# A decoder step on one core: where VectorE's low parts stand beside side work, and when TensorE's side steps are issued

## The chip, the core and the metric

The kernel runs on one core of one Trainium2 chip. The metric is the device time of one execution in microseconds (us), the median of several runs. The core's engines run side by side, each through its own queue in order: TensorE (PE in the profile; PEld is its weight load), VectorE (DVE), ScalarE (ACT), GpSimd (POOL) and SyncE (SP), which here only starts transfers. An instruction that waits holds up whatever stands behind it in the same queue.

## The reference, cut to what matters

One layer of a hybrid decoder for 256 prompt tokens and 8 x 4 sample tokens (288 in all), width 2048, in fp32:

```python
mkv = rms_norm(mem_prompt, mem_norm_g) @ w_mem_kv            # keys and values of 256 memory tokens
h = rms_norm(x, norm_g)
c_h, c_b, c_c, c_g, q, n_g, b_g, kv6, m_q, m_g = split_cols(h @ w_in)
y_a = silu(c_g) * short_conv_mixer(c_h, c_b, c_c, conv_prev, w_conv)
# 8 query heads, 2 key groups: compressed, selected and sliding-window attention
o_cmp, o_sel = nsa_cmp_sel(q, q_rot, pos, k_cmp, v_cmp, k_sel, v_sel)   # sample: over 2048 cached rows
y_b = silu(n_g) * (g0 * o_cmp + g1 * o_sel + g2 * o_win)
y_m = silu(m_g) * gqa_attend(m_q, mem_k, mem_v)              # 4 heads over the memory
x = x + concatenate([y_a, y_b, y_m]) @ w_out
y = rms_norm(x, final_g)
```

The new key and value rows, the convolution state and the updated windows are outputs too.

## The kernel before, in words

**The weight products.** Columns of a weight matrix are taken 128 at a time; each such tile has 16 blocks of 128 rows and is cut into two *halves* of 8 blocks (128 x 1024 numbers, 512 KB). There are 152 halves (`NH`): 16 of `w_mem` (the first four multiply raw fp32, the `zf` products, `DIRECT = 4`), 104 of `w_in`, and 32 of `w_out` in two passes of 16. The *first output pass* (halves 120 to 135) takes the rows that belong to convolution and memory attention (`y1a`, `y1b`); the *last pass* (halves 136 to 151) takes those of the sparse attention (`y`), and there each half is a whole product.

To keep fp32 precision a half `s` is split: ScalarE copies it to a *high part* `wh` (`w_hi`), VectorE subtracts that from the raw half and writes the *low part* `wl` (`w_lo`). A half then takes 24 matmuls into a PSUM tile `z` (two buffers): 8 with `wh` times the high part of the tokens, 8 with `wh` times their low part, 8 with `wl`; they are sorted so that `wl` is wanted from the 17th on (in halves 4 and 5 earlier). Raw halves have 5 buffers (`WR`), high parts 3, low parts 2. A raw buffer is free once its low part is written, and then GpSimd's queue starts the load of a later half (`w_load`, `LOAD_AT`). So `wl` of half s+2 can be written only when the matmuls of half s are over.

**Side work.** Everything else (norms, rotary embedding, convolution, gates, all attention, pooling of the cached rows, outputs) is written as Python generators. `chunk()` runs after every 12 matmuls of a half and once after each product; it advances each generator in the list `live` to its next `yield`. `yield 1` means the next chunk, `yield 2` the one after. All engines' queues are thereby written out in one order by hand, ahead of time.

**The planner.** While the program is written, `at[0]` adds up estimates for TensorE, `at[VEC]` and `at[ACT]` for the other engines' work, `at[1]` for transfers. `until(i)` lets a generator go on only when `at[0]` has passed the end of engine `i`'s work so far by `WAIT`. `behind(i, j)` puts one engine's clock behind another's and issues nothing. These estimates steer the order alone; what runs is governed by semaphores.

**The stream of cached rows.** `stage_stream` takes the stages in a fixed order as their tiles arrive: `cmp_use` (pooling one tile: a multiplication shared by VectorE and GpSimd, then a sum `pooled` on VectorE; 64 of them), `selk_use` and `wink_use` (scores `sk`), `memk_use` (scores `smd`), `memv_use` (`omd`), `winv_use` and `selv_use` (outputs `od`). `cmp_use` is held back while VectorE's clock is more than `BACKLOG` ahead of TensorE's. `selk_use` waits for the flag `q`, `memk_use` for `mq`. Six buffers `st` (and later one more, `qk`) hold the tiles.

**Steps that the change and the prediction name.** `first_tiles` runs the first four halves and splits the memory tokens (`m`); `mem_tile` scales `z` into `mvt`; `prep_x` normalises and splits the tokens. `dec_cmp` makes compressed scores (`sc`) and, from `S`, the block importances (`imp`); `dec_softmax` builds `odr` from `S` and transposes it (`pe`); `dec_out` and `mem_out` transpose the collected outputs (`ot`, `otm`). `prompt_cmp` makes the prompt's compressed scores (`kcps`, `scp`, `scpt`) and weights `pc`, which `prompt_nsa` transposes (`pct`) before its own softmax `P` and its transposition `pt`. `split_y1` makes the inputs of the first output pass once `prompt_done` and `mem_decoded` are set, `split_y2` and `split_decode` those of the last; if they are not there, the program idles.

In the last pass `second_pass` adds `z` to `ysum` on VectorE, squares it on ScalarE (`ysq`), adds the square to `yacc` on VectorE and scales `ysum` on ScalarE; `residual` adds the input `xr` meanwhile. For half s the queues hold, in this order, ScalarE: `wh` of s+2, then square and scale of s; VectorE: `wl` of s+2, then the sum and the accumulation of s.

Of the kernel before, what the change touches and what calls it, by code (L numbers as in the profile page):

```python
# [47 lines left out]
C_SEL = C_NS + 32  # L48
CS = C_SEL + 2048
CMP_LAG = 2  # L50
WAIT = 0.2
BACKLOG = 2.5
NST = 6

T_C0, T_C1, T_K0, T_V0 = (24, 94), (94, 185), (67, 113), (128, 162)
# [12 lines left out]
LOAD_AT = 21  # L68
DIRECT = 4
WARM = 5  # L70
TAIL_BUSY = (5, 7)
OUT_PIECES = (1, 2, 2, 3, 3, 3, 2)

# [2 lines left out]
def decode_step(ctx, tc, xT, xN, memT, cst, w_in, w_mem, w_out, w_bg, pt, ptv, ckc, ckk, ckv, wk, wv, mk, mv,  # L76
# [22 lines left out]
    VEC, ACT, SYNC = 2, 3, 4  # L99
# [38 lines left out]
    def behind(i, j):  # L138

        at[i] = max(at[i], at[j])  # L140
# [79 lines left out]
    def w_hi(s):  # L220
        if DIRECT <= s < NH and s not in his:
            his[s] = pw.tile([128, 1024], F32R, name=f"wh{s}", tag="wh", bufs=WH)
            act.activation(his[s], raws[s], AF.Copy)
# [18 lines left out]
    def product_half(out, hi, lo, first, last):  # L242
        s = nhalf[0]
        nhalf[0] += 1
        w_hi(s + 2)
        wh, wl = his.pop(s), los.pop(s)
        mm = []
        for j in range(8):
            a = wh[:, j * 128:(j + 1) * 128]
            mm += [(j, a, hi(j)), (j + (0 if s > DIRECT + 1 else 4), a, lo(j)), (j + 8, wl[:, j * 128:(j + 1) * 128], hi(j))]  # L250
        mm.sort(key=lambda x: x[0])
        for n, (_, a, b) in enumerate(mm):
            if s == DIRECT and n == 0:
                w_load(s + WR)
            if n == LOAD_AT:
                w_load(s + WR + 1)
            matmul(out, a, b, start=(first and n == 0), stop=(last and n == 23))
            if n == 23:
                w_lo(s + 2)
            if n % 12 == 11 and not (last and n == 23):  # L260
                chunk()
# [3 lines left out]
    def first_tiles():  # L265


        z = [pz.tile([128, 512], F32, name=f"zf{i}", tag="z")[:, :256] for i in range(2)]
        for k0 in (0, 8):
            for i in range(2):  # L270
                s = nhalf[0]
                nhalf[0] += 1
                w_hi(s + 2)
                w_lo(s + 1)
                w = raws[s]
                for j in range(8):
                    matmul(z[i], w[:, j * 128:(j + 1) * 128], m_g(k0 + j, 1)[:, 0], start=(k0 + j == 0), stop=(k0 + j == 15))
                    if j == 7:
                        w_load(s + WR)
                        first_loads(s)  # L280
                        if s == DIRECT - 1:
                            w_lo(s + 2)
                    if j == 3 or j == 7 and k0 == 0:
                        chunk()
                if i == 1:
                    for k in (k0, k0 + 4):
                        vec.tensor_tensor(m_hl[1][:, k:k + 4, :], m_g(k, 4), m_hl[0][:, k:k + 4, :].bitcast(F32),
                                                op=ALU.subtract)
                if k0 == 8:
                    yield z[i]  # L290
# [78 lines left out]
    def dec_cmp(hf):  # L369

        yield from until(VEC)
        while ("S", hf) not in env or hf and "first" not in env:
            yield 1
        t = ptr.tile([128, 512], F32, name=f"kcT{hf}", tag="t")
        matmul(t[:, :256], wcmp[:, 0], pooled[hf][:, 0].rearrange("p g q b n -> p (g q b n)"), start=True, stop=True)
        kcT = zt("A", "kcT")[:, :256].rearrange("p (g n) -> p g n", g=2)
        vec.tensor_copy(kcT.rearrange("p g n -> p (g n)"), t[:, :256])
        yield 1
        t = ptr.tile([128, 512], F32, name=f"vc{hf}", tag="t")
        for g in range(2):  # L380
            matmul(t[:, g * 128:(g + 1) * 128], pooled[hf][:, 1, g].rearrange("p q b n -> p (q b n)"), wcmp[:, 1], start=True, stop=True)
        act.activation(Vc, t[:, :256], AF.Copy)
        yield 1
        S = env["S", hf]
        s = pss.tile([128, 512], F32, name=f"sc{hf}", tag="s")
        for g in range(2):
            for b in range(4):
                matmul(s[32 * b:32 * b + 32, 0:32], qcols(1, 4 * hf + b, g), kcT[:, g].rearrange("p (q b n) -> p q b n", q=8, b=4)[:, :, b, :],
                                 start=(g == 0), stop=(g == 1), skip_group_check=True)
        mx, nm, sm = small(1, "mx1"), small(1, "nm1"), small(1, "sm1")  # L390
        vec.tensor_reduce(mx, s[:, 0:32], axis=AX.X, op=ALU.max)
        vec.tensor_scalar(nm, mx, -SCALE, None, op0=ALU.mult)
        yield 1
        act.activation(S[:, 0:32], s[:, 0:32], AF.Exp, scale=SCALE, bias=nm, accum_out=sm)
        yield 1
        vec.reciprocal(sm, sm)
        vec.tensor_scalar(S[:, 0:32], S[:, 0:32], sm, None, op0=ALU.mult)
        yield 1
        t = ptr.tile([128, 512], F32, name=f"imp{hf}", tag="t")
        matmul(t[:, 0:32], C("rep"), S[:, 0:32], start=True, stop=True)  # L400
        imp = small(32, "imp", 1)
        vec.tensor_copy(imp, t[:, 0:32])
        yield 1
        v8, v16 = small(8, "v8"), small(8, "v16")
        iv = imp[:, 1:31]
        vec.max(v8, iv)
        vec.match_replace(iv, v8, iv, -2.0)
        vec.max(v16, iv)
        vec.memset(v16[:, 5:8], -3.0)
        vec.match_replace(iv, v16, iv, -2.0)  # L410
        madd = small(32, "madd", 1)
        vec.tensor_scalar(madd, imp, -1.0, NEG, op0=ALU.is_ge, op1=ALU.mult)
        vec.memset(madd[:, 0:1], 0.0)
        vec.memset(madd[:, 31:32], 0.0)
        env["madd", hf] = madd
        spawn(dec_softmax(hf), 1)
# [48 lines left out]
    def dec_softmax(hf):  # L465
# [32 lines left out]
        for a, b, m in ((C_NS, h, 1), (h, CS, 1), (C_WIN, C_NS, 2)):  # L498
            vec.tensor_scalar(S[:, a:b], S[:, a:b], sm[:, m:m + 1], None, op0=ALU.mult)
            if m == 1:  # L500
# [5 lines left out]
        vec.tensor_tensor(X.rearrange("p (q b n) -> p q b n", q=8, b=4),  # L506
                                S[:, 0:32].rearrange("p (q n) -> p q n", q=8).unsqueeze(2).to_broadcast([128, 8, 4, 4]),
                                C("bsel").unsqueeze(1).unsqueeze(3).to_broadcast([128, 8, 4, 4]), op=ALU.mult)
        yield 1
        t = ptr.tile([128, 512], F32, name=f"pe{hf}", tag="t")  # L510
        transpose(t[:, 0:128], X, ident)
        env.pop("odr")
# [64 lines left out]
    def dec_out(hf):  # L577
        yield from take("odr")
        o = env.pop("o")
        mg = C("mg")  # L580
        r = small(128, "odr", 1)
        vec.tensor_scalar(r, o[:, 0:128], mg[:, 0:1], None, op0=ALU.mult)
        vec.scalar_tensor_tensor(r, o[:, 128:256], mg[:, 1:2], r, op0=ALU.mult, op1=ALU.add)
        yield 2
        t = ptr.tile([128, 512], F32, name=f"ot{hf}", tag="t")
        transpose(t[:, 0:128], r, ident)
        env.pop("odr")
        a, b = 256 + 16 * hf, 272 + 16 * hf
        act.activation(mixed[:, 8:16, a:b].rearrange("p h (b t) -> p h b t", t=4),
                             t[:, 0:128].rearrange("p (b h t) -> p h b t", b=4, t=4), AF.Copy)  # L590
        env["decoded", hf] = True
# [65 lines left out]
    def mem_out():  # L657
        yield from take("odr")
        o, mh = env["mo"], C("mh")
        env.pop("o")  # L660
        r = small(128, "odr", 1)
        vec.tensor_scalar(r, o[:, 0:128], mh[:, 0:1], None, op0=ALU.mult)
        for h in range(1, 4):
            vec.scalar_tensor_tensor(r, o[:, h * 128:(h + 1) * 128], mh[:, h:h + 1], r, op0=ALU.mult, op1=ALU.add)
        yield 2
        t = ptr.tile([128, 512], F32, name="otm", tag="t")
        transpose(t[:, 0:128], r, ident)
        env.pop("odr")
        act.activation(mixed[:, 4:8, 256:NT].rearrange("p h (b t) -> p h b t", t=4),
                             t[:, 0:128].rearrange("p (b h t) -> p h b t", b=8, t=4), AF.Copy)  # L670
        env["mem_decoded"] = True
# [313 lines left out]
    def q_tile(h, z):  # L985
# [12 lines left out]
        if hh == 3:  # L998
            yield 1
            yield from rope_out(put)  # L1000
        if h == 7:
            env["q"] = True

    pool_p = one.tile([128, 2, 2, 4], F32, name="pool_p")
# [36 lines left out]
    def mq_tile(h, z):  # L1041
        act.activation(mq[:, h, :], z[:, :256], AF.Copy)
        sv = z[:, 256:NT].rearrange("p (c b t) -> p c b t", b=2, t=4)
        for b2 in range(2):
            o = b2 * 16 + h * 4
            vec.tensor_copy(qmz[:, :, b2, h, o:o + 4], sv[:, :, b2, :])
        if h == 3:
            env["mq"] = True
        return
        yield  # L1050
# [104 lines left out]
    def prompt_cmp():  # L1155
# [12 lines left out]
        v = vcp.rearrange("p g d -> p (g d)")  # L1168
        act.activation(v, t[0:96, 128:384], AF.Copy)
        vec.tensor_tensor(v[32:64], t[32:64, 128:384], v[32:64].bitcast(F32), op=ALU.subtract)  # L1170
        yield 2

        s = pss.tile([128, 512], F32, name="scp", tag="s")
        for i in range(4):
# [1 line left out]
                   stop=True, skip_group_check=True)  # L1176
        sT = pbig.tile([128, 1024], F32, name="scpT", tag="big")
        act.activation(sT[:, :512], s, AF.Copy)
        yield 1
        t = ptr.tile([128, 512], F32, name="scpt", tag="t")  # L1180
        for i in range(4):
            transpose(t[:, i * 128:(i + 1) * 128], sT[:, i * 128:(i + 1) * 128], ident)
# [19 lines left out]
        for a in range(2):  # L1202
            vec.tensor_tensor(pc3[:, a], pc[:, a].unsqueeze(1).to_broadcast([128, 3, 8, 4]),
                                    smv[:, a].unsqueeze(1).unsqueeze(3).to_broadcast([128, 3, 8, 4]), op=ALU.mult)
        yield 1

    def prompt_nsa(g, tt):
        L = 128 * (tt + 1)
# [351 lines left out]
```

## Time and profile before

| | before |
|---|---|
| runs, us | 641.89, 642.78, 643.66 (median 642.78) |
| profiled execution, us | 642.73, of which the span of instructions is 641.0 |
| granted TensorE clock | 0.99 |
| TensorE busy | 609.3 us, 95% of the span |
| VectorE busy | 457.5 us, 71% |
| ScalarE busy | 287.9 us, 45% |
| GpSimd busy | 206.8 us, 32% |
| moved by DMA | 188.40 MB, mean 294 GB/s |

How to read the lines that follow: a line of the order of time gives start and length in us, engine, line of the kernel, operation, tiles (written `<-` read), shape and count, and in brackets how long the engine had been idle before it and what ended that. Matmuls are pipelined, so a line of 16 of them overlaps the next. A line of waits gives the total in us, how many, and the longest. A line of stretches gives for each engine the busy time and the number of instructions, then the granted clock of TensorE, the share of the DMA engines in use and GB/s.

The stages by time: memory projection to 67 us (with the tokens' preparation in 40 to 64), queries, keys and values, convolution and gates with all attention beside them to 508 us, first output pass to 569 us, last pass to 628 us, final norm and output to the end.

### The profile page before, as it was taken

To read this page: it belongs to the slowest core of one execution; us is meant where nothing else is said; L and a number is where in the kernel's file an instruction comes from. 1 tells how busy PE (TensorE), PEld (TensorE's weight loads), DVE (VectorE), ACT (ScalarE), POOL (GpSimd) and SP (SyncE) were. 2 spreads that over 40 slices of the span, in tenths; PEclk is the share of its full clock that TensorE was granted. 3 is DMA by queue.
4 is the path that set the end of the run, shared out by engine and by line. 5 is a ranking of instruction groups with operands and counts; after the bars stand their busy time and mean duration, and the time that the engine had idled before them with its cause. 6 is when DMAs were issued, how large, how long until landed. Compare 5 with 4: busy or idle time off the path is not lost. (4 is left out here: it accounts for less than half of the span.)

```text
span 641.0 us, 13356 instructions
## 1 busy us (share of the span) xinstructions
PE 609.3 (95%) x4895; PEld 561.3 (88%) x4895; DVE 457.5 (71%) x735; ACT 287.9 (45%) x500; POOL 206.8 (32%) x288
## 2 busy tenths in 40 slices
PE   7899999999999999889999899999999999999983
PEld 5799999989999899878898789988889889999973
DVE  3769799979587679677786978977586443447554
ACT  4656444454454434233334443445434343435550
POOL 1122554534236433232364452322103343122100
PEclk9999999999999999889999999999999999999998
DMA  8999698999999997877778899898979997488703
GB/s 260 360 404 399 211 359 303 337 328 327 314 286 357 383 379 264 327 249 259 266 281 269 292 342 296 295 321 293 372 265 341 336 300 291 152 299 261 230 4 147
DMA packets 74627, 188.40 MB, mean 294 GB/s; under 512 B 8945, under 2 KB 25842, under 8 KB 74178
## 3 DMA queue, kind: packets, MB, share of 16 engines
q0 software_dynamic: 27232, 105.10, 46.7%
q1 hardware_dynamic: 46320, 81.17, 36.4%
q10 hardware_dynamic: 1010, 1.28, 0.5%
q8 instruction: 38, 0.62, 0.4%
q14 instruction: 27, 0.22, 0.1%
HBM read 182.31 MB, written 13.60 MB: 306 GB/s over the span
## 5 line engine op out<-in xcount | busy, mean ns | idle before, releaser
L133 DVE TENSOR_TENSOR wl<-w,wh 128x1024 fp32r<-128x1024 f32 x148 | 184.4, 1247 | 110.9 <-PE z L116 50.9
L116 PE MATMUL z<-x,wh 128*128 128x288 f32 x1664 | 258.4, 304 | 0.4 <-ACT wh L133 0.4
L116 PEld LDWEIGHTS z<-x,wh 128*128 128x128 f32 x1664 | 232.5, 190 | 9.2 <-issue 6.9
L133 ACT ACTIVATE wh<-w 128x1024 fp32r<-128x1024 f32 x148 | 154.6, 1051 | 24.0 <-PE z L116 17.6
L116 PE MATMUL z<-x,wl 128*128 128x288 f32 x832 | 127.0, 295 | 0.2 <-DVE wl L133 0.2
L116 PEld LDWEIGHTS z<-x,wl 128*128 128x128 f32 x832 | 115.7, 188 | 0.4 <-DVE wl L133 0.4
L341 POOL TENSOR_TENSOR st<-st,cst 128x512 f32<-128x512 f32 x56 | 63.0, 1126 | 129.2 <-issue 55.3
L217 POOL DMA_DIRECT2D w<-w_in x104 | 58.3, 560 | 93.6 <-DVE wl L133 73.3
L133 DVE TENSOR_REDUCE pooled<-st 128x16 f32<-128x1024 f32 x56 | 67.8, 1211 | 8.6 <-POOL st L341 8.6
L116 PE MATMUL z<-y,wh 128*128 128x288 f32 x256 | 37.8, 299 | 3.5 <-DVE ysum L133 3.5
L133 DVE TENSOR_TENSOR st<-st,cst 128x512 f32<-128x512 f32 x56 | 39.0, 699 | 2.7 <-DMA st<-ckc 2.7
L561 POOL DMA_INDIRECT st<-ckv,rows_v x29 | 30.6, 1055 | 31.4 <-PE od L116 14.9
L116 PEld LDWEIGHTS z<-y,wh 128*128 128x128 f32 x256 | 34.8, 188 | 5.7 <-issue 5.6
L217 POOL DMA_DIRECT2D w<-w_out x32 | 17.6, 553 | 61.2 <-DVE wl L133 57.7
L116 PE MATMUL z<-y1a,wh 128*128 128x288 f32 x224 | 35.4, 298 | 0.0
L116 PEld LDWEIGHTS z<-y1a,wh 128*128 128x128 f32 x224 | 31.8, 188 | 1.6 <-issue 1.2
L116 PE MATMUL z<-m,wh 128*128 128x256 f32 x192 | 27.4, 287 | 3.3 <-DVE m L133 1.6
L133 ACT ACTIVATE P<-P,nm 128x128 f32<-128x128 f32 (+1 forms) x32 | 14.2, 444 | 32.2 <-DVE nm L133 32.2
L116 PEld LDWEIGHTS z<-m,wh 128*128 128x128 f32 x192 | 24.5, 191 | 4.5 <-issue 1.9
L133 ACT ACTIVATE ysum<-z 128x288 f32<-128x288 f32 x16 | 6.6, 412 | 32.1 <-PE z L116 32.1
L133 ACT ACTIVATE se<-z 128x288 f32<-128x288 f32 x16 | 6.6, 412 | 31.2 <-PE z L116 31.2
L116 PE MATMUL sk<-st,qz 128*32 128x256 f32 x288 | 19.8, 382 | 0.0
(274 smaller groups left out, 715.0 us busy)
## 6 DMA issues: line engine op xcount, KB each, us to landing
w<-w_in POOLq DMA_DIRECT2D x104, 512.0 KB, 6.2
st<-ckc SPq DMA_DIRECT2D x112, 256.0 KB, 6.0
w<-w_out POOLq DMA_DIRECT2D x32, 512.0 KB, 5.1
st<-ckk SPq DMA_DIRECT2D x112, 128.0 KB, 5.2
w<-w_mem POOLq DMA_DIRECT2D x11, 512.0 KB, 9.1
o_wk<-wk POOLq DMA_DIRECT2D x8, 512.0 KB, 6.3
o_wv<-wv POOLq DMA_DIRECT2D x8, 512.0 KB, 6.6
qk<-ckc SPq DMA_DIRECT2D x16, 256.0 KB, 6.4
```

What stands on the lines that cost most here:

```text
L116: nc.tensor.matmul(out, a, b, **kw)
L133: return getattr(self.engine, name)(*args, **kw)
L217: (nc.gpsimd if s >= WR else nc.sync).dma_start(raws[s], wsrc[s])
L341: done.append(eng.tensor_tensor(tm[:, :, kv], tm[:, :, kv], acmp[:, kv].unsqueeze(1).unsqueeze(1).to_broadcast([128, 2, 4, 64]), op=ALU.mu ...
L561: nc.gpsimd.indirect_dma_start(t, None, ckv, bass.IndirectOffsetOnAxis(ap=rows_v[:, j * 4 + b:j * 4 + b + 1], axis=0))
```

## The change: what it does

1. *Low parts.* Before, `wl` of half s+2 is issued right after the last matmul of half s, ahead of the side work of that chunk. Now this holds only for s from 22 (`LOW_FIRST`) to 133 (`NH - 18`, not included). Every half begins with `w_lo(s + 1)`, which does nothing if that part is there; so in halves before 22 and from 134 on, the low part is issued one product or chunk later, behind the side work. The extra call at the end of the four direct halves is gone.
2. *Waits for estimates.* Ten places where a generator went on after one or two chunks now use `until`: in `dec_cmp` before `sc` and before `imp`, in `dec_softmax` before `pe`, in `dec_out` and `mem_out` before the transposition, in `prompt_cmp` before `scp`, before `scpt` and at its end (before `pct`), and before the flags `q` and `mq` are set. Two `behind` lines chain the clocks around an exponential.
3. *Constants.* `WAIT` goes from 0.2 to 0.8, `BACKLOG` from 2.5 to 1.6.

```diff
-WAIT = 0.2
-BACKLOG = 2.5
+WAIT = 0.8
+BACKLOG = 1.6
...
+LOW_FIRST = 22
...
 def product_half(out, hi, lo, first, last):
         w_hi(s + 2)
+        w_lo(s + 1)
         wh, wl = his.pop(s), los.pop(s)
...
-            if n == 23:
+            if n == 23 and LOW_FIRST <= s < NH - 18:
                 w_lo(s + 2)
             if n % 12 == 11 and not (last and n == 23):
                 chunk()
...
 def first_tiles():
                         first_loads(s)
-                        if s == DIRECT - 1:
-                            w_lo(s + 2)
...
 def dec_cmp(hf):
         act.activation(Vc, t[:, :256], AF.Copy)
-        yield 1
+        yield from until(VEC)
...
         yield 1
+        behind(ACT, VEC)
         act.activation(S[:, 0:32], s[:, 0:32], AF.Exp, scale=SCALE, bias=nm, accum_out=sm)
         yield 1
+        behind(VEC, ACT)
         vec.reciprocal(sm, sm)
         vec.tensor_scalar(S[:, 0:32], S[:, 0:32], sm, None, op0=ALU.mult)
-        yield 1
+        yield from until(VEC)
         t = ptr.tile([128, 512], F32, name=f"imp{hf}", tag="t")
...
 def dec_softmax(hf):                       # after odr, before pe
-        yield 1
+        yield from until(VEC)
...
 def dec_out(hf) and mem_out():             # after odr, before ot and otm
-        yield 2
+        yield from until(VEC)
...
 def q_tile(h, z):
         if h == 7:
+            yield from until(VEC)
             env["q"] = True
...
 def mq_tile(h, z):
         if h == 3:
+            yield from until(VEC)
             env["mq"] = True
...
 def prompt_cmp():
         vec.tensor_tensor(v[32:64], t[32:64, 128:384], v[32:64].bitcast(F32), op=ALU.subtract)
-        yield 2
+        yield from until(VEC)
...
         act.activation(sT[:, :512], s, AF.Copy)
-        yield 1
+        yield from until(ACT)
...
                                     smv[:, a].unsqueeze(1).unsqueeze(3).to_broadcast([128, 3, 8, 4]), op=ALU.mult)
-        yield 1
+        yield from until(VEC)
```

More of the change, by code (lines that the diff above doesn't have):

```diff
@@ L1170, in prompt_cmp @@
         vec.tensor_tensor(v[32:64], t[32:64, 128:384], v[32:64].bitcast(F32), op=ALU.subtract)
-        yield 2
+        yield from until(VEC)
         s = pss.tile([128, 512], F32, name="scp", tag="s")
@@ L1204, in prompt_cmp @@
                                     smv[:, a].unsqueeze(1).unsqueeze(3).to_broadcast([128, 3, 8, 4]), op=ALU.mult)
-        yield 1
+        yield from until(VEC)
     def prompt_nsa(g, tt):
```

## The prediction

> **What bounds the kernel now.** I read the busy shares and the clock row of the page first, then who TensorE waited for, then stretches cut at the stages, and last the order of time around each wait.
>
> ```profile
> span 641.0 us, 13356 instructions
> PE 609.3 (95%) x4895; PEld 561.3 (88%) x4895; DVE 457.5 (71%) x735; ACT 287.9 (45%) x500; POOL 206.8 (32%) x288
> PEclk9999999999999999889999999999999999999998
> ```
>
> TensorE carries the span, so only what stops or slows it counts; VectorE has room on the whole. The clock digits fall to 8 in two slices of the middle, which is taken up below. Who TensorE waited for (total us, times, longest):
>
> ```profile
> PE z L116 <- DVE ysum L133: 3.5, 10, 1.7
> PE pe L121 <- DVE odr L133: 3.1, 1, 3.1
> PE pt L121 <- DVE P L133: 2.6, 2, 2.0
> PE pct L121 <- DVE pc L133: 2.0, 1, 2.0
> PE imp L116 <- DVE S L133: 1.7, 2, 1.2
> PE z L116 <- DVE m L133: 1.6, 1, 1.6
> PE z L116 <- DVE mvt L133: 0.9, 1, 0.9
> ```
>
> Each of these waits is for VectorE, although VectorE is not full: work that TensorE needs stands behind other work in its queue. By stage (stretch, length, then PE busy and instructions; the last three figures are clock, DMA share, GB/s):
>
> ```profile
> 24.20:67.20 43.00, 40.08 (x334) 37.62 (x335) 33.98 (x56) 27.27 (x42) 10.69 (x20) 1.00 1.00 373
> 150.00:508.30 358.30, 348.83 (x2918) 316.49 (x2917) 270.07 (x453) 152.72 (x289) 125.50 (x166) 0.99 0.88 308
> 508.30:569.20 60.90, 60.90 (x527) 56.67 (x527) 25.51 (x28) 26.39 (x41) 19.73 (x28) 1.00 0.75 254
> 585.30:627.60 42.30, 38.44 (x271) 36.13 (x271) 23.80 (x36) 22.66 (x36) 5.02 (x10) 1.00 0.40 130
> ```
>
> The idle time of TensorE lies in three places: 2.9 us in the tokens' preparation, 9.5 us in the long middle, 3.9 us in the last pass. The first output pass (508 to 569) has none.
>
> **The change, term 1: the last pass.** Its order of time:
>
> ```profile
> 572.46 2.33 PE L116 MATMUL z<-y,wh 128*128 128x288 f32 x16
> 575.66 2.29 PE L116 MATMUL z<-y,wh 128*128 128x288 f32 x16
> ...
> 585.21 0.44 ACT L133 ACTIVATE ysq<-ysum 128x288 f32<-128x288 f32 x1 [1.66 <-DVE ysum L133]
> 585.32 2.36 PE L116 MATMUL z<-y,wh 128*128 128x288 f32 x16
> 585.68 0.54 ACT L133 ACTIVATE ysum<-ysum,cst 128x288 f32<-128x288 f32 x1
> 586.13 1.04 ACT L133 ACTIVATE wh<-w 128x1024 fp32r<-128x1024 f32 x1
> 587.20 1.23 DVE L133 TENSOR_TENSOR wl<-w,wh 128x1024 fp32r<-128x1024 f32 x1 [0.69 <-ACT wh L133]
> 588.35 0.45 DVE L133 TENSOR_TENSOR ysum<-z,ysum 128x288 f32<-128x288 f32 x1
> 588.94 2.34 PE L116 MATMUL z<-y,wh 128*128 128x288 f32 x16 [0.21 <-DVE ysum L133]
> 623.04 1.83 PE L116 MATMUL z<-y,wh 128*128 128x288 f32 x12 [1.69 <-DVE ysum L133]
> 625.26 0.83 PE L116 MATMUL ssqy<-cst,yacc 128*128 128x1 f32 x6 [0.39 <-DVE yacc L133]
> ```
>
> Undisturbed, a half tile takes 575.66 - 572.46 = 3.20 us. From 585.32 it takes 588.94 - 585.32 = 3.62 us, and that is a ring over two engines: square (ysq), scale, high part (wh) on ScalarE, then low part (wl), sum (ysum) on VectorE, then the next square. It closes because the low part of two halves ahead is issued before the sum of this half, and the sum frees the z buffer that TensorE wants. From 585.32 to 623.04 there are ten halves in 37.72 us; ten at 3.20 are 32.0, so the ring costs 5.7 us. (1.69 us of it is one wait, where ScalarE loads a table.)
>
> From half 134 on the change issues the low part at the start of the next half, behind sum, square and accumulation. The ring is then cut: the sum waits for TensorE alone. What VectorE does for one half, after the product's end:
>
> ```profile
> L133 DVE TENSOR_TENSOR yacc<-yacc,ysq 128x288 f32<-128x288 f32 x14 | 6.4, 457 | 5.2 <-ACT ysq L133 5.1
> L133 DVE TENSOR_TENSOR ysum<-ysum,xr 128x864 f32<-128x864 f32 x4 | 4.2, 1048 | 0.0
> ```
>
> Sum 0.45, then accumulation 0.46 behind the square of 0.44, then the low part 1.23: about 2.7 us with hand-overs, and some 3.1 us in the four halves with a residual addition of 1.05, part of which runs beside the square. Both are under 3.20, and the low part is needed only after 16 matmuls (2.1 us) of the half after the next. ScalarE has 0.44 + 0.54 + 1.04 = 2.0 us a half, and once the table load (the wait of 1.69 us is its mark), which a whole half of lead covers. Behind the later low part stands the weight load in GpSimd's queue, for that raw buffer; it is wanted four halves (12.8 us) on and takes 5.1 us:
>
> ```profile
> w<-w_out POOLq DMA_DIRECT2D x32, 512.0 KB, 5.1
> ```
>
> Without that lead it would cost up to 3 us a half. The extra piece in the last half (ssqy, 0.39 us of waiting) stays, and may grow by 0.2, since the last accumulation then ends about 1.6 us after the product before, when TensorE arrives there. Term 1: -5.7 + 0.2 = **-5.5 us**.
>
> **Term 2: steps that wait for estimates, and WAIT and BACKLOG.** No instruction is added; ten steps that came one or two chunks after their VectorE or ScalarE work (a chunk is 12 matmuls, 1.6 us) now also wait until the planner's clock of that engine is passed by 0.8 us, and the steps that had this already wait 0.8 instead of 0.2. The largest case:
>
> ```profile
> 257.71 1.21 DVE L133 TENSOR_REDUCE pooled<-st 128x16 f32<-128x1024 f32 x1
> 258.84 0.33 DVE L133 TENSOR_TENSOR odr<-S,cst 128x128 f32<-128x128 f32 x1
> 259.22 0.33 PE L121 MATMUL pe<-cst,odr 128*128 128x128 f32 x1 [3.11 <-DVE odr L133]
> ```
>
> The transposition pe was issued one chunk after odr, which stood behind pooling work. Two chunks later it finds odr ready, and the 3.11 us are filled with projection matmuls. The same holds for pct (2.0) behind a chain of small operations that the planner does count. The granted clock tells what else these two waits cost:
>
> ```profile
> 260.00:265.00 5.00, 5.00 (x29) 5.00 (x28) 1.49 (x3) 2.73 (x4) 0.53 (x1) 0.66 1.04 404
> 280.00:285.00 5.00, 2.96 (x20) 2.75 (x19) 4.90 (x13) 2.19 (x5) 1.61 (x2) 0.89 0.68 243
> 285.00:290.00 5.00, 5.00 (x32) 4.98 (x31) 3.40 (x5) 2.09 (x4) 2.12 (x3) 0.77 0.72 235
> 620.00:624.00 4.00, 2.31 (x18) 2.10 (x17) 2.18 (x4) 2.24 (x5) 0.00 (x0) 1.00 0.00 0
> ```
>
> Behind the wait of 3.1 us the clock is 0.66 over 5 us: 1.7 us lost. Behind the wait of 2.0 us it is 0.89 and 0.77: 0.55 + 1.15 = 1.7 us lost. The wait of 1.69 us in the last pass (620 to 624) lowers nothing. So both go with their waits: 3.4 us. The Trainium skill, "TensorE: Matmul & The Clock Gate", Part 1 (What's actually happening), puts the fall to half rate behind at least one whole idle window of about 3.4 us; by that neither wait would be long enough, the 3.4 us would not come back with them, and the sum would be 629.9 instead of 626.5. The trace disagrees for the wait of 2.0 us, so the rows decide.
>
> At most this term holds 3.1 + 2.0 + 1.7 + 2.6 + 3.4 = 12.8 us. I take pe, pct and their clock whole (8.5), 1.2 of imp (one of its two waits follows a VectorE stall that no estimate of VectorE knows), and half of pt (1.3), which was guarded at 0.2 already and waited all the same: 11.0 us. Against it, all side work behind moves to other places and meets other queues. That is not in the trace; between nothing and the whole 12.8 us again, I take 1.5 us, nearest to pt, where guarded steps still waited 2.6 us in all. Term 2: **-9.5 us**.
>
> The lateness itself (a step one or two chunks later, pooling held back by BACKLOG, the flags q and mq set later) I cost at nothing: TensorE always has projection matmuls to put in its place. The cover ends where the first output pass needs its split inputs:
>
> ```profile
> 502.78 0.21 DVE L133 TENSOR_TENSOR y1b<-mixed,y1a 128x64 fp32r<-128x64 f32 x1
> L116 PE MATMUL z<-y1a,wh x224: 288/295/402, 508.4 to 567.9; 128*128 128x288 f32 x112
> ```
>
> The last split ends 503.0, the pass starts 508.4: 5.4 us, three chunks of lateness; each chunk beyond costs 1.6 us.
>
> **Term 3: the tokens' preparation (halves before 24).** Here too the low part goes behind side work.
>
> ```profile
> 27.42 1.22 DVE L133 TENSOR_TENSOR wl<-w,wh 128x1024 fp32r<-128x1024 f32 x1 [1.45 <-ACT wh L133]
> 28.56 2.35 DVE L133 TENSOR_TENSOR m<-mixed,m 128x1024 fp32r<-128x1024 f32 x2
> 29.83 1.22 PE L116 MATMUL z<-m,wh 128*128 128x256 f32 x8 [1.64 <-DVE m L133]
> ```
>
> The low part of half 5 waited 1.45 us for its high part and held up m. Behind m, it lets m start at 27.42 - 1.45 = 25.97, and the wait of 1.64 goes; the low part then ends at 25.97 + 2.35 + 1.22 = 29.5, while TensorE wants it at about 29.2, so 0.4 us come back: -1.2. The wait for mvt (0.9) may shrink too, but DMA is full here (share 1.00 above) and earlier TensorE asks for weights earlier. Bounds -2.5 (both gone) and +1 (low parts late for GpSimd's weight loads, the size of mvt). I take **-1.2 us**.
>
> **Sum.** The profiled execution took 642.73 us (span 641.0), the median of the runs 642.78, so one base serves. 642.7 - 5.5 - 9.5 - 1.2 = **626.5 us**.
>
> **Rivals.**
> - *All waits go*: 642.7 - 5.7 - 12.8 - 2.5 = 621.7. For it: every wait has a guard now. Against: imp and pt.
> - *The middle's waits come back elsewhere*: term 2 is nothing, 642.7 - 5.5 - 1.2 = 636.0. For it: the same VectorE work must be done, and pt was guarded and waited.
> - *Too few z buffers, not the order*: the last pass keeps its 3.62 us, 626.5 + 5.5 = 632.0. For it: TensorE's wait there is for a buffer that ysum frees. Against: the first output pass uses the same two buffers at 3.2 us a half with no idle time. The Trainium skill, "Perfetto Trace Analysis", Identifying Performance Opportunities, reads a gap that repeats on the busy engine as a sign of too few buffers; the trace speaks for the order.
> - *The low clock has another cause*: 626.5 + 3.4 = 629.9.
> - *Slower*: the guarded chain to the memory outputs comes so late that the first output pass waits for its inputs. Slower than 644.7 it becomes once the 16.2 us are used up and 2 more: 18.2 / 1.6 = 11 chunks beyond the three that are free. Two or three late steps stand in that chain, so it would take pooling held back for some 20 us.
> - *The guards do nothing* (estimates already past) and the ring re-forms at 3.6 us: within 0.3% of 642.8.
>
> **Chances.** Forecast 0.60, all gone 0.10, middle back 0.14, buffers 0.05, clock 0.03, no change 0.03, slower 0.05. Faster by over 0.3% (about 2 us, what this kernel's measurement can tell) sums to 0.92, within it 0.03, slower 0.05. The range for 8 in 10 reaches from 621.0 (all gone, a little over) to 636.5 (middle back).
>
> **What would show it.** Last pass: halves at 3.20 us to the end, no TensorE wait for ysum, wl behind yacc on VectorE. Middle: no waits of pe and pct and no half-rate clock before the end. Early: no wait for m. Wrong it would be if TensorE idles between the gates and the first output pass, if waits for P or sk grow, or if the last pass stays above 3.4 us a half.

## The result, and the profile after

The changed kernel takes 626.16 us (median of 4 runs, 624.2 to 627.6) against 643.22 us before (4 runs): a ratio of 0.9735, 95% interval 0.9701 to 0.977. Run again later, beside other runs of the kernel before (641.96 us), it took 623.90 us, ratio 0.9735 (0.9699 to 0.977). The forecast was 626.5.

The page of the profiled execution (625.25 us in all):

```profile
span 622.8 us, 13340 instructions
PE 604.3 (97%) x4895; PEld 558.4 (90%) x4895; DVE 458.2 (74%) x735; ACT 287.2 (46%) x500; POOL 209.4 (34%) x288
PEclk9999999999999999999999999999999999999997
```

VectorE does the same 735 instructions in the same time; TensorE is idle less, and the clock digits have no 8 in the middle any more. Who TensorE waited for (total us, times, longest):

```profile
PE z L117 <- ACT wh L134: 2.2, 3, 1.2
PE sk L117 <- DMA st<-ckk: 2.2, 3, 1.2
PE zeros L117 <- POOL zeros L783: 1.1, 1, 1.1
PE zf L117 <- DVE mixed L134: 1.0, 2, 0.8
PE zf L117 <- DMA w<-w_mem: 1.0, 1, 1.0
PE acc L117 <- ACT cu L134: 0.5, 1, 0.5
PE z L117 <- DVE wl L134: 0.5, 2, 0.3
```

All seven waits that the prediction listed are gone (ysum, odr, P, pc, S, m, mvt). The waits for zeros, mixed and w_mem stand at the very start and were there before (1.1, 1.7 and 1.6 us). What came in is smaller: 1.9 of the 2.2 us for wh (0.4 was there before), 2.2 for the transfer of sk's rows, 0.5 for acc and 0.3 for wl. Where the time went, by the stages' own marks: four stretches from the first split product to the first token product, to the first output pass, to the last pass, to its last `wl` matmuls; first before, then after (stretch, length, then the engines' busy times in the order PE, PEld, DVE, ACT, POOL, then clock, DMA share, GB/s).

```profile
24.25:67.24 42.99, 40.11 (x334) 37.66 (x335) 33.93 (x56) 27.26 (x42) 10.68 (x19) 1.00 1.00 373
67.24:508.40 441.16, 431.07 (x3547) 396.85 (x3546) 345.51 (x566) 192.20 (x356) 164.16 (x214) 0.99 0.89 309
508.40:569.25 60.85, 60.85 (x527) 56.62 (x526) 25.51 (x28) 26.39 (x41) 19.62 (x28) 1.00 0.75 254
569.25:627.50 58.25, 54.38 (x392) 51.97 (x391) 34.27 (x49) 29.91 (x47) 8.38 (x16) 1.00 0.55 182
```

```profile
22.27:64.10 41.83, 39.69 (x337) 37.49 (x337) 34.72 (x59) 27.34 (x42) 11.18 (x20) 1.00 1.03 392
64.10:496.67 432.57, 429.14 (x3546) 394.20 (x3545) 345.45 (x564) 191.72 (x356) 166.40 (x213) 1.00 0.90 316
496.67:557.42 60.75, 60.75 (x527) 56.52 (x526) 26.40 (x29) 26.22 (x41) 20.04 (x29) 1.00 0.76 252
557.42:609.30 51.88, 51.88 (x391) 51.72 (x390) 33.39 (x48) 29.88 (x47) 8.35 (x16) 1.00 0.63 207
```

The preparation is 1.2 us shorter, the middle 8.6, the first output pass 0.1, the last pass 6.4. Another 2.0 us stand ahead of the first mark (24.25 to 22.27), where both kernels wait, among other things, for their first transfers; in the eleven other profiles that mark lies between 22.9 and 25.2, with the early part of the change and without it, so these 2 us belong to the execution and not to the change. Together 18.2 us between these two profiled spans, 17.1 between the medians.

The last pass in order of time, one half:

```profile
567.04 2.29 PE L117 MATMUL z<-y,wh 128*128 128x288 f32 x16
567.24 0.46 DVE L134 TENSOR_TENSOR ysum<-z,ysum 128x288 f32<-128x288 f32 x1 [0.27 <-PE z L117]
567.73 0.45 ACT L134 ACTIVATE ysq<-ysum 128x288 f32<-128x288 f32 x1 [1.23 <-DVE ysum L134]
568.21 0.46 DVE L134 TENSOR_TENSOR yacc<-yacc,ysq 128x288 f32<-128x288 f32 x1 [0.51 <-ACT ysq L134]
568.59 1.22 DVE L134 TENSOR_TENSOR wl<-w,wh 128x1024 fp32r<-128x1024 f32 x1
570.24 2.29 PE L117 MATMUL z<-y,wh 128*128 128x288 f32 x16
605.44 1.76 PE L117 MATMUL z<-y,wh 128*128 128x288 f32 x12
607.12 0.83 PE L117 MATMUL ssqy<-cst,yacc 128*128 128x1 f32 x6
```

The sum now waits for TensorE, not the reverse. From 567.04 to 605.44 there are twelve halves in 38.40 us, 3.20 each, to the end, and the extra piece ssqy is reached without a wait for yacc.

### The profile page after: what moved, and what is told of

It reads as the page before. It is cut to its first block, busy times and chain, and to the rows that moved or that the text cites. A ratio compares the mean times of both kernels' runs of the same rounds, so it can differ in the third digit from the quotient of the medians.

```text
span 622.8 us, 13340 instructions
## 1 busy us (share of the span) xinstructions
PE 604.3 (97%) x4895; PEld 558.4 (90%) x4895; DVE 458.2 (74%) x735; ACT 287.2 (46%) x500; POOL 209.4 (34%) x288
## 4 chain that ended last, share of the span: by engine, by line
PE 83%; DMA 10%; DVE 3%; ACT 1%; issue 1%; SPq 1%; ACTq 0%; DVEq 0%
PE z L117 67%; DMA st<-ckk 4%; PE od L117 3%; DMA st<-xN 2%; PE sk L117 2%; PE acc L117 2%; PE s L117 1%; DMA mraw<-memT 1%; DMA st<-ckc 1%; DMA qk<-ckk 1%; PE pv L122 1%; DVE ysum L134 1%; DMA rows_v<-ptv 1%; PE pt L122 1%; PE omd L117 1%
## 5 line engine op out<-in xcount | busy, mean ns | idle before, releaser
L117 PE MATMUL z<-x,wh 128*128 128x288 f32 x1664 | 255.1, 302 | 0.4 <-ACT wh L134 0.4
L117 PEld LDWEIGHTS z<-x,wh 128*128 128x128 f32 x1664 | 229.9, 188 | 9.5 <-issue 7.3
L341 POOL TENSOR_TENSOR st<-st,cst 128x512 f32<-128x512 f32 x56 | 64.8, 1160 | 117.5 <-issue 55.4
L218 POOL DMA_DIRECT2D w<-w_out x32 | 17.5, 551 | 58.6 <-DVE wl L134 44.8
L117 PE MATMUL sk<-st,qz 128*32 128x256 f32 x288 | 21.6, 382 | 2.2 <-DMA st<-ckk 2.2
L117 PE MATMUL z<-y,wl 128*128 128x288 f32 x128 | 19.6, 295 | 0.0
```

Of the source, the lines that this page charges most:

```text
L117: nc.tensor.matmul(out, a, b, **kw)
L218: (nc.gpsimd if s >= WR else nc.sync).dma_start(raws[s], wsrc[s])
L341: done.append(eng.tensor_tensor(tm[:, :, kv], tm[:, :, kv], acmp[:, kv].unsqueeze(1).unsqueeze(1).to_broadcast([128, 2, 4, 64]), op=ALU.mu ...
```

## The experiments

All are compared with runs of the kernel before on the same chip, taken together with them. Single executions of one kernel lie up to 5 us from their median here, so differences under 2 us are read from the traces, each of which shows one execution.

**The parts alone.** First the last pass only:

```diff
         w_hi(s + 2)
+        w_lo(s + 1)
...
-            if n == 23:
+            if n == 23 and s < NH - 18:
```

> The kernel before with one part of the change: in the last pass (halves from 134 on) the low part goes behind the side work. Theory (the order closes a ring over ScalarE and VectorE): the ten halves at 3.62 us go back to 3.20, no wait of TensorE for ysum is left, time 5.5 to 6.5 us less. Rival (two z buffers are too few): halves stay at 3.6 us, time unchanged within 1 us.

Measured 636.22 us against 642.06, ratio 0.9917 (0.9882 to 0.9952); in its profile the last pass starts at 567.1 and its last `wl` matmul at 619.0, 51.9 us later, as in the changed kernel. No wait for ysum is left. The order closes the ring; the number of z buffers is the same, so it alone does not hold the halves at 3.62 us.

Then the early part only (the same `w_lo(s + 1)`, then `if n == 23 and s >= 22`, and the extra call in `first_tiles` taken out):

> The kernel before with one part of the change: before half 24 the low part goes behind the side work. Theory: the wait for m (1.6 us) goes and the stretch from the first split product to the first token product is 1 to 1.5 us shorter, time about 1.2 us less. Rival (DMA is full there): the waits turn into waits for weights, time unchanged within 0.5 us.

Measured 639.01 us, ratio 0.995 (0.9916 to 0.9983), which is 3.1 us less with an interval from 1 to 5. The trace gives the stretch before the first token product 41.8 us, 1.2 less than before; the wait for m is replaced by this one (waits of TensorE in this run):

```profile
PE z L116 <- ACT wh L133: 1.8, 2, 1.5
```

So the theory holds in direction. Its size is less sure: in four other profiles with the old early part and full clock the same stretch takes 42.1 to 42.7 us, which leaves 0.3 to 0.9. No trace shows where the rest of the 3.1 us came from. Of the new wait 1.5 us are for one high part. It does not wait for weights; it stands in ScalarE's queue behind squares of token rows. One of those squares waited 1.13 us for its rows, so the rival, that DMA is full there, has a part in it.

Then the ten guards only, with the old constants:

> The kernel before with one part of the change: the ten new waits for estimates and the two lines that chain clocks, with the old constants 0.2 and 2.5 and the old order of low parts. Theory: these guards carry term 2; the waits for odr (3.1) and pc (2.0) and the half-rate clock behind them go, time 6 to 9 us less. Rival (the constants carry it): under 3 us less, and TensorE still waits over 1.5 us for odr or pc.

Measured 635.52 us, ratio 0.9899 (0.9868 to 0.9929), 6.5 us less. Its waits:

```profile
PE pt L122 <- DVE P L134: 2.0, 1, 2.0
PE pe L122 <- DVE odr L134: 1.5, 1, 1.5
PE imp L117 <- DVE S L134: 1.2, 1, 1.2
```

The wait for pc is gone, that for odr is halved: with 0.2 us of margin the planner lets pe go 1.5 us too early. And the constants only:

> The kernel before with one part of the change: the two constants 0.8 and 1.6 alone. Theory: steps without a guard still come one chunk after their work, so pe and pct still wait, only pt (2.6 us of waiting) gains: 1 to 3 us less. Rival (less pooling queued on VectorE is enough): over 5 us less and no wait over 1 us for odr or pc.

Measured 639.98 us, ratio 0.997 (0.9938 to 1.0003): 2.1 us less, not clear of nothing. Its waits:

```profile
PE pct L121 <- DVE pc L133: 2.9, 1, 2.9
PE acc L116 <- DVE pcT L133: 2.3, 1, 2.3
PE pe L121 <- DVE odr L133: 0.9, 1, 0.9
PE pt L121 <- DVE P L133: 0.9, 1, 0.9
```

Two thirds of the odr wait went without a guard, which neither theory had; less pooling in front is the likely reason, but both constants were changed here, so it is not shown. The wait for pc grew, and a new one of 2.3 us came elsewhere. The four parts add up to 5.8 + 3.1 + 6.5 + 2.1 = 17.5 us, the whole measured 17.1. That is closer than the parts allow: each has an interval some 4 us wide, and of the 3.1 the trace shows 1.2 at most.

**The ring by itself.** The kernel before, low parts untouched; only the scaling leaves the ring:

```diff
+        if n < 14:
+            yield 1
         act.activation(y, y, AF.Copy, scale=C("fg")[:, n:n + 1])
```

> The kernel before, low parts where they were; in the last pass ScalarE's scaling of ysum (0.45 us in the ring) is issued half a half later, behind the high part, for the first 14 tiles. Theory (the ring square, scale, high part, low part, sum sets 3.62 us): without scale it is 3.62 - 0.45 = 3.17 us, under the 3.20 of TensorE, so the halves go to 3.20 and time falls by 5 to 6.3 us, as much as with the low part behind. Rival (the place of the low part itself matters, by the two low-part buffers or the z buffers): halves stay over 3.5 us, under 1.5 us less.

Measured 636.15 us, ratio 0.9884 (0.9842 to 0.9926): 5.9 us less. In order of time:

```profile
586.80 2.29 PE L116 MATMUL z<-y,wh 128*128 128x288 f32 x16
587.05 1.23 DVE L133 TENSOR_TENSOR wl<-w,wh 128x1024 fp32r<-128x1024 f32 x1 [0.27 <-ACT wh L133]
588.19 0.45 DVE L133 TENSOR_TENSOR ysum<-z,ysum 128x288 f32<-128x288 f32 x1
588.68 0.45 ACT L133 ACTIVATE ysq<-ysum 128x288 f32<-128x288 f32 x1 [1.38 <-DVE ysum L133]
589.03 1.04 ACT L133 ACTIVATE wh<-w 128x1024 fp32r<-128x1024 f32 x1
590.00 0.56 PE L116 MATMUL z<-y,wh 128*128 128x288 f32 x3
```

The halves are 590.00 - 586.80 = 3.20 us with the low part still in front of the sum, and no wait for ysum is left. So it was the length of the ring, and either link may be taken out.

**The clock.** The kernel before, with TensorE kept at work (results unused) in the two longest waits:

```diff
+            fill(t, 22)          # first pe: 22 matmuls of 128x288
         transpose(t[:, 0:128], X, ident)
...
+            fill(t, 16)          # first pct: 16
```

> The kernel before, with 22 extra matmuls of 128x288 (results unused) issued ahead of the first pe and 16 ahead of the first pct, so that TensorE works through the two waits of 3.1 and 2.0 us instead of idling. Nothing else moves. Theory (these two waits lower the clock in many executions, 3.4 us at half rate each time): mean granted clock up from about 0.990 to 0.993 or more, time 1.5 to 3.4 us less although work was added. Rival (the half-rate stretches come from elsewhere or by chance): clock and time unchanged within 1 us, or 0.5 us more.

Measured 640.04 us against 642.09, ratio 0.9975 (0.9949 to 1.0001): 2.1 us less with 38 matmuls more; the median of the granted clock went from 0.991 (17 executions) to 0.994 (12). That agrees with the theory, though the interval of the time just reaches 1. But the loss is not tied to the waits one to one. The run with the last pass alone has the same waits for odr and pc. In order of time, first a line of the kernel before, then this run with its stretches:

```profile
264.68 2.30 PE L116 MATMUL z<-x,wh 128*128 128x288 f32 x16
```

```profile
259.43 0.33 PE L121 MATMUL pe<-cst,odr 128*128 128x128 f32 x1 [3.11 <-DVE odr L133]
263.40 2.30 PE L116 MATMUL z<-x,wh 128*128 128x288 f32 x16
282.41 0.29 PE L121 MATMUL pct<-cst,pc 128*96 128x128 f32 x1 [2.03 <-DVE pc L133]
257.00:262.00 5.00, 2.57 (x20) 2.58 (x21) 4.63 (x6) 1.98 (x4) 2.14 (x3) 1.00 1.02 407
262.00:267.00 5.00, 5.00 (x40) 5.00 (x39) 1.90 (x5) 1.06 (x1) 0.69 (x2) 1.00 1.03 397
283.00:288.00 5.00, 5.00 (x39) 4.97 (x38) 4.87 (x7) 3.33 (x6) 2.12 (x3) 1.00 0.78 261
```

The clock stays 1.00 behind both. From pe to the second group of 16 matmuls behind it TensorE takes 263.40 - 259.43 = 3.97 us here, and before the change 264.68 - 259.22 = 5.46 for the same work. With the late scaling, the same wait goes with a half-rate stretch twice as long:

```profile
258.98 0.48 PE L121 MATMUL pe<-cst,odr 128*128 128x128 f32 x1 [3.12 <-DVE odr L133]
265.60 2.28 PE L116 MATMUL z<-x,wh 128*128 128x288 f32 x16
255.00:265.00 10.00, 6.88 (x33) 6.62 (x32) 6.19 (x8) 2.94 (x6) 2.88 (x5) 0.66 1.03 406
```

0.66 over 10 us is 6.8 us at half rate, where before it was 3.4. It begins at 258.2, inside the wait, where half rate costs nothing, and the same work takes 265.60 - 258.98 = 6.62 us. So one and the same wait cost nothing, 1.5 or 2.65 us in these three executions. Over the 57 executions of the kernel before that ran beside these experiments, the mean granted clock lies between 0.982 and 0.996 with a median of 0.990; the 14 with 0.993 or more have a median time of 639.3 us, the 23 under 0.989 one of 643.5.

**Low parts behind the side work everywhere.** The changed kernel without its condition for the middle:

```diff
-            if n == 23 and LOW_FIRST <= s < NH - 18:
-                w_lo(s + 2)
```

> The changed kernel with low parts behind the side work in all halves, in the long middle too. Theory (in the middle VectorE's side work stands up to 5 us deep, so low parts come late): TensorE waits for wl, over 5 us in all, and the time is 3 to 10 us above the changed kernel's 626. Rival (a low part in front only makes VectorE idle until TensorE frees the buffer, 45 us of that in the trace): 1 to 3 us under 626.

Measured 626.09 us, ratio to before 0.9725 (0.9684 to 0.9766), against 626.16 for the changed kernel beside its own runs of before. Neither theory: TensorE does wait for low parts now,

```profile
PE z L117 <- DVE wl L134: 3.5, 4, 2.0
```

and for P (1.4) again; the waits for acc and for wh in the preparation are smaller or gone. TensorE is idle 6.1 us of the middle instead of 3.4, and yet the middle takes 433.4 us (65.0 to 498.4) beside 432.6, because its busy time is 1.9 us less; no run here shows why. That the low parts stay in front in the middle is worth nothing that these runs can tell.

**The constants inside the changed kernel.** Both old (0.2 and 2.5), then WAIT alone old (0.2):

> The changed kernel with the old constants, WAIT 0.2 and BACKLOG 2.5. Theory (parts add up; alone the constants gave 2.1 us): 628 to 629, with waits for odr, P or S of 1 to 2 us back. Rival (the constants do only what the guards do already): 626 to 627, no difference to the changed kernel beyond 1 us.

> The changed kernel with WAIT back at 0.2 and BACKLOG at 1.6. Theory (the longer wait is what covers the planner's error, which was 1.5 to 2.4 us for odr and P with the old constants): 628 to 629, like with both old constants. Rival (less pooling queued ahead is what covers it): 626 to 627.

Measured 629.08 us (ratio to before 0.9775, 0.9733 to 0.9817) and 626.56 us (0.9777, 0.973 to 0.9823; the changed kernel measured beside it took 623.90 us, 0.9735). With both old, P (2.4) and odr (1.5) wait again; with the old WAIT alone as well:

```profile
PE pt L122 <- DVE P L134: 2.3, 1, 2.3
PE pe L122 <- DVE odr L134: 1.5, 1, 1.5
```

Both waits that the longer WAIT covers come back whatever BACKLOG is, which speaks for the first theory. In time, both old constants lie 2.9 us above the changed kernel's 626.16, which was measured beside other runs; the old WAIT alone, whose 626.56 would by itself fit the rival, lies 2.7 above the 623.90 measured beside it. The intervals overlap, so the waits are the evidence here and the times agree with it.

**Again, and with later squares.** The changed kernel once more, and with `XSQ_AT = (6, 6, 9, 10, 12, 12)` in place of `(6, 6, 9, 9, 10, 10)`:

> The changed kernel once more, for a second look at its waits and clock and as base for the run with later squares. Both theories: 625 to 628 us, mean granted clock 0.994 to 0.995, no wait of TensorE for odr, pc, m or ysum.

> The changed kernel with ScalarE's last two squares of the token rows issued two chunks later (and one of the others one chunk), so that the high part of half 8 stands ahead of them. Theory (the wait of 1.25 us of TensorE for wh near 33 us is ScalarE's queue): the wait goes, 1 to 1.3 us less than the changed kernel in the same call. Rival (DMA is full there, and the weights or the token norm come late instead): within 0.5 us of it, with a new wait for w, mixed or x before 70 us.

Measured 623.90 us, 1.1 under the expected range, with none of the four waits and a median clock of 0.9945; and 623.27 us, ratio 0.9717 (0.9681 to 0.9754) to before. The waits for wh in the preparation are gone with the later squares, but they are gone in the second profile of the changed kernel too, where the first split product began later (25.2 us) and no square waited more than 0.3 us for its rows. (The 0.4 us for wh that both still show stand near 126 us, and stood there before the change.) The step is not told from nothing.

## Why the prediction was right, point by point

**Term 1, the last pass (-5.5):** right in mechanism, a little small. The trace gives -6.4 for the stretch, the part alone -5.8. Ten halves brought the 5.7 forecast; the term that was mis-sized is ssqy, put at +0.2. From the first matmul of the last half to ssqy it is 2.22 us before (623.04 to 625.26) and 1.68 after (605.44 to 607.12), 0.5 less. With the late scaling it is 1.68 too, with the low parts where they were: the 0.39 us of waiting came from the lateness that the ring had built up, so they went with the ring. The rival of too few z buffers is refuted by two runs.

**Term 2, the middle (-9.5):** -8.6 by the trace, 6.5 + 2.1 by the parts, and two errors in it partly cancel. Waits: pe and pct went as forecast; imp and pt went whole, where 1.2 of 1.7 and 1.3 of 2.6 were taken. The new waits were larger than the 1.5 allowed: 2.2 us for the scores sk, 0.5 for acc. Together that is 9.4 - 2.7 = 6.7 us less idle time, where 7.6 - 1.5 = 6.1 were forecast. The clock was put too high, as the next point shows. The prediction looked for new waits on VectorE; the larger one is for a transfer, two thirds of it here:

```profile
208.20 0.59 PE L117 MATMUL sk<-st,qz 128*32 128x256 f32 x2 [0.29 <-DMA st<-ckk]
210.02 0.81 PE L117 MATMUL sk<-st,qz 128*32 128x256 f32 x9 [1.23 <-DMA st<-ckk]
```

The prediction had named growing waits for sk as a sign of being wrong, and this one came, from none to 2.2 us. All six profiles of the changed kernel and its variants have such a wait (1.0 to 3.0 us). Of the seven others only the run with the last pass alone has one:

```profile
PE sk L116 <- DMA st<-ckk: 1.3, 1, 1.3
```

There the stalls ahead of it (m 1.5, mvt 0.9) are still in place, and from the issue of the first of these loads to the first score it is 17.4 us, as in the kernel before, beside 17.0 in the changed kernel. So earlier use of the rows is not enough to explain it, and the cause stays open.

**The clock (3.4 of term 2):** that half rate follows these waits is right, but the price was too high. In the run with the early part alone the middle has nearly the same waits (odr 3.1, P 2.6, pc 2.0, S 1.6) at full clock:

```profile
66.20:504.50 438.30, 428.41 (x3546) 394.26 (x3545) 345.64 (x564) 192.27 (x356) 165.70 (x214) 1.00 0.90 311
```

That is 2.9 us less than the 441.16 before, and so near the price of the two half-rate stretches in the profiled execution; between before and after, TensorE's busy time in the middle fell by 1.9 us. On the average the clock went from 0.990 to 0.995, which over 641 us is the forecast 3.2, but the mean counts idle time too (the clock is 0.50 at the end of both profiles, when no matmul runs), and the fill brought 2.1 us. The step that failed is that each of the two waits has a fixed price: the same wait of 3.1 us cost nothing, 1.5 or 2.65 us in three profiles. The Trainium skill, "TensorE: Matmul & The Clock Gate", Part 1, says that the activity window is free-running; that fits a price that changes from one execution to the next. Its condition of a whole idle window of about 3.4 us is not met here: waits of 3.1 and 2.0 us were followed by half rate. The prediction weighed only the latter.

**Term 3, the preparation (-1.2):** -1.2 between these two profiles, but 0.3 to 0.9 where the early part alone is set beside other profiles of the old early part, so the size is not settled. The wait for m is gone. In its place came 1.9 us (0.60 and 1.25) of waiting for wh in the first profile of the changed kernel and none in the second, and 0.3 us for the low part, where 0.4 was forecast: ScalarE's queue, not VectorE's, was the new limit. The wait for mvt went too, which was not counted.

**Lateness at no cost:** right. The last split input was ready at 491.3, the first output pass began at 496.7, still 5.4 us. The slower rival had its place there, and nothing of it was seen.

## What to carry to other kernels

When two engines hand each other work in a loop, add up the loop from the rows and compare it with the engine that should be the bound; if the loop is longer, move any one link out of it, whichever is easiest, since here the low part or the scaling each gave the whole 6 us. A side step on the bounding engine should be issued only when its input is ready with a margin over the planner's error; 0.2 us left waits of 1.5 to 2.4 us, 0.8 removed them. Once such stalls are gone, look at the transfers next: the largest new wait in the middle was for one.

## What the runs showed of the hardware that was not expected

The half-rate stretches of TensorE differ from execution to execution: 3.4 us each, once 6.8, at waits of 1.7 to 3.1 us that in other executions cost nothing. The shortest was the wait of 1.66 us for m in the run with late scaling, with one of 0.94 us shortly ahead of it; the wait of 1.69 us in the last pass, from which the prediction took a limit, was not followed by any. These stretches go with a good part of the spread of this kernel's times (over the 57 executions the time falls by 2.4 us for each 0.005 of clock, a straight line through them).
